# The first modulation rows as four 32-column tiles, with all tokens normed first

## The chip, the cores and the metric

The kernel runs on one core of one Trainium2 chip. The metric is the device time in microseconds (us) of one execution, the median of several runs. The core has five engines that run side by side and wait for one another through semaphores: PE (TensorE: matrix products and transposes), DVE (VectorE), ACT (ScalarE), POOL (GpSimd) and SP (SyncE). In this kernel SP issues nearly all transfers, one after the other in its queue, and ACT issues some small ones.

## The reference, cut to what matters

One inference step of a two-layer diffusion trunk: 512 latent tokens and 128 context tokens, width 1024, float32. Layer 0 is neighbourhood attention, layer 1 grouped-query attention; each is followed by a gated feed-forward part with a width-3 convolution. Everything that the change touches is the start of layer 0, up to its values:

```python
def adaln(cond, w, b):
    m = jax.nn.silu(cond) @ w + b
    return jnp.split(m[..., None, :], 6, axis=-1)
...
        sh_ap, sc_ap, g_ap, sh_fp, sc_fp, g_fp = adaln(c_ctx, ada_w[l], ada_b[l])
        sh_as, sc_as, g_as, sh_fs, sc_fs, g_fs = adaln(c, ada_w[l], ada_b[l])
        hp = rmsnorm(xp, norm_mix_pre[l]) * (1.0 + sc_ap) + sh_ap
        hs = rmsnorm(xs, norm_mix_pre[l]) * (1.0 + sc_as) + sh_as
        if l % N_MIXERS == 0:
            qp, kp, vp = na_qkv(hp, na_w_qkv[i])
...
            qs, ks_, vs = na_qkv(hs, na_w_qkv[i])
```

So two condition vectors (one for latents, one for context) are multiplied with a 1024 x 6144 matrix. The first 2048 columns of the result are the shift and the scale of the first norm. With them the normed tokens become the input of the query, key and value products.

## The kernel before

All names below are those of the code. Tokens are held as five tiles of 128 (`NT`), four latent and one context. The width of 1024 is eight blocks of 128 (`KC`).

**The first stage** does four things. It loads the five token tiles and norms them (`x_load`, `x_norm`: square on ACT, two small POOL operations, scaling on DVE). It transposes them on PE into `xT` (`x_turn`, eight transposes a tile). It forms the shift and scale (`mod_load`, `mod_rows`, `mod_cols`) and applies them to `xT`. The scaled result is held twice: `hT[0]` is rounded to the reduced type F32R, which PE multiplies in one pass, and `hT[1]` is the remainder. Last come the values of the first four heads (`v_part`), in three products for each block: high by high, high by low, low by high.

**The modulation goes in four groups** (`i` = 0 to 3). Group `i` holds 256 columns of the shift and 256 of the scale, which belong to two of the eight blocks of `xT`. Its weights are four tiles of 128 x 4 x 256 numbers, 512 KB each. A constant string says what becomes of each tile: `r` keeps it in float32 and multiplies it by `stf` (the conditions in float32, four stationary columns), `p` and `d` split it by `wsplit` into a rounded part (a cast on ACT) and a remainder (a subtraction, on POOL for `p`, on DVE for `d`), and multiply both parts by `st` and `st2`:

```python
ADA0 = "rrpdprdr" * 2
```

`mod_rows(i)` leaves four rows of 512 numbers in one PSUM bank; ACT copies them out as `rs`. `mod_cols(i)` multiplies pieces of `rs` by the small selector `sel`, which turns rows into columns and adds up the pieces, then forms `gcol` and `hcol` on DVE and scales: ACT writes `hT[0]`, DVE overwrites `xT` and subtracts to get `hT[1]`. `v_part(i, cs)` then uses the two blocks of group `i` for the token tiles in `cs`: six products for each of them.

**The order.** PE keeps the order in which the code issues its instructions (`mm`, `turn` and `pe` chain them). The other engines' order is made by a scheduler that follows the code's order as priority. Buffers carry a tag with a number of copies; a load into a tag waits until one of its buffers is given back, and all later loads in SP's queue wait behind it. Today the raw tiles have six buffers (`wf`), and the splits draw on four shared ones (`wr`, `wh`, `wl`), which the value and query-key weights of the next stage use too. The value weights are loaded by `wv_load` between the groups.

**What follows.** `crs` are convolution weights, loaded on ACT's queue and turned on PE just ahead of the last `v_part`. The next stage, neighbourhood attention, begins with query-key products (PE records named `qk`), builds bias tables for each head on POOL (`tb`, from transfers named `tr`), and fills PE's time with the later modulation rows (`ada_work`, records named `ada`), which already use four stationary tiles of 32 columns:

```python
for j in range(4):
    mm(ps[32 * j : 32 * j + 32, 0:256], scolp[:, 2 * kk : 2 * kk + 32], raw[:, 256 * j : 256 * j + 256],
       start=kk == 0, stop=kk == KC - 1)
```

`scolp` holds the conditions of block k in columns 2k and 2k + 1; of the 32 columns that a tile reads from there, only the first two are used.

Of the kernel before, what the change touches and what calls it, by code (L numbers as in the profile page):

```python
# [9 lines left out]
F32 = mybir.dt.float32  # L10
# [31 lines left out]
NC = 3  # L42
QKH = (slice(0, 256), slice(256, T))
CTX = 2
ADA0 = "rrpdprdr" * 2
ORDER = "a f a f p0 t0 a s0 f s1 t1 a f v0 t2 a a f a v1 f p1 f a a s2 a s3 v2 f f f a a p2 f f".split()
ORDER2 = "t0 p0 s0 s1 f a f a f f t1 v0 t2 a a f a f f a a p1 v1 s2 a f a s3 f v2 f p2 a f f".split()
PRO = 19
# [43 lines left out]
def hybrid_step(ctx: ExitStack, tc: tile.TileContext, A, O):  # L92
# [10 lines left out]
    def mm(*a, **k):  # L103
        pe(nc.tensor.matmul(*a, **k))  # L104
# [4 lines left out]
    def f32(t):  # L109
        return t.bitcast(F32)  # L110
# [39 lines left out]
    def wsplit(src, a, b, low=None, own=None, pin=False):  # L150
        q = own or wp
        raw = q.tile([P, a, b], F32, tag="wr", name="wr")
        nc.sync.dma_start(raw, src)
        hi = q.tile([P, a, b], F32R, tag="wh", name="wh")
        i = nc.scalar.copy(hi, raw)  # L155
        lo = q.tile([P, a, b], F32R, tag="wl", name="wl")
        j = (low or nc.vector).tensor_sub(lo, raw, f32(hi))  # L157
        if pin:
            tc.keep_in_program_order(i)
            tc.keep_in_program_order(j)  # L160
        return hi, lo

    def rows(w, r0, nr, c0, ncol):
        return w[r0 * P : (r0 + nr) * P, c0 : c0 + ncol].rearrange("(k p) n -> p k n", p=P)
# [282 lines left out]
    vts_of = {}  # L447
    with ExitStack() as s:
        sp = s.enter_context(pool("st"))
        sel = sp.tile([4, 2], F32, name="sel")  # L450
        nc.sync.dma_start(sel, A["k_sel"])
        xts = []

        def x_load(t):
# [11 lines left out]
        colb = sp.tile([P, 24], F32, name="colb")  # L466
        nc.vector.tensor_copy(colb, ct[:, 16:40])
        bk.put(ct)
        st = sp.tile([P, KC, 4], F32R, name="st1")
        st2 = sp.tile([P, KC, 4], F32R, name="st2")  # L470
        stf = sp.tile([P, KC, 4], F32, name="stf")
        nc.vector.tensor_copy(st2, zero_f.unsqueeze(2).broadcast_to([P, 8, 4]))
        nc.vector.tensor_copy(stf, zero_f.unsqueeze(2).broadcast_to([P, 8, 4]))
        for q in range(2):
            sc8 = scol[:, 8 * q : 8 * q + 8]
            nc.vector.tensor_copy(st[:, :, 2 * q], sc8)
            nc.vector.tensor_copy(st2[:, :, 2 * q], sc8)
            nc.vector.tensor_copy(stf[:, :, 2 * q], sc8)
            nc.vector.tensor_copy(scolp[:, q : 2 * KC : 2], sc8)
            nc.vector.tensor_sub(st[:, :, 2 * q + 1], sc8, f32(st[:, :, 2 * q]))  # L480
        xT = sp.tile([P, KC, T], F32, name="xT")
        gcol = sp.tile([P, KC, 2], F32, name="gcol")
        hcol = sp.tile([P, KC, 2], F32, name="hcol")
# [20 lines left out]
                bk.put(tr)  # L504

        def mod_load(i):
            out = []
            for j in range(4):
                src = rows(A["ada_w"][0], 4 * (j % 2), 4, D - D * (j // 2) + 256 * i, 256)
                how = ADA0[4 * i + j]  # L510
                if how == "r":
                    raw = sp.tile([P, 4, 256], F32, tag="wf", name="wf", bufs=6)
                    nc.sync.dma_start(raw, src)
                    out.append((raw,))
                else:
                    out.append(wsplit(src, 4, 256, nc.gpsimd if how == "p" else None))
            return out

        def mod_rows(i, ws):

            row = bk.get("row")
            for j, w in enumerate(ws):
                rv = row[0:4, 256 * (j // 2) : 256 * (j // 2) + 256]
                for k in range(4):
                    kk = 4 * (j % 2) + k
                    for x, y in zip((stf,) if len(w) == 1 else (st, st2), w):
                        mm(rv, x[:, kk, :], y[:, k, :], start=kk == 0 and y is w[0],
                           stop=kk == KC - 1 and y is w[-1])
            rs = sp.tile([4, 512], F32, tag="rs", name="rs")
            nc.scalar.copy(rs, row[0:4, :])  # L530
            bk.put(row)
            return rs

        def mod_cols(i, rs):

            col = bk.get("col")
            for n in range(4):
                mm(col[:, 2 * n : 2 * n + 2], rs[:, n * P : n * P + P], sel, start=True, stop=True)
            cv = col[:, 0:8].rearrange("p (a b) -> p a b", b=2)
            ks = slice(2 * i, 2 * i + 2)  # L540

            def bc(c0):
                return colb[:, c0 + 2 * i : c0 + 2 * i + 2].unsqueeze(2).broadcast_to([P, 2, 2])

            nc.vector.scalar_tensor_tensor(gcol[:, ks, :], cv[:, 0:2, :], 1.0, bc(8), op0=ALU.add, op1=ALU.add)
            nc.vector.tensor_mul(gcol[:, ks, :], gcol[:, ks, :], bc(16))
            nc.vector.tensor_add(hcol[:, ks, :], cv[:, 2:4, :], bc(0))
            bk.put(col)
            for k in (2 * i, 2 * i + 1):
                for q, cs in ((0, slice(0, NS)), (1, slice(NS, T))):  # L550
                    g1, h1 = gcol[:, k, q : q + 1], hcol[:, k, q : q + 1]
                    nc.scalar.activation(hT[0][:, k, cs], xT[:, k, cs], AF.Identity, bias=h1, scale=g1)
                    nc.vector.tensor_scalar(xT[:, k, cs], xT[:, k, cs], g1, h1, op0=ALU.mult, op1=ALU.add)
                nc.vector.tensor_sub(hT[1][:, k, 0:T], xT[:, k, :], f32(hT[0][:, k, 0:T]))
# [7 lines left out]
        def x_in_norm(ts):  # L562
            for t in ts:
                x_load(t)
                x_norm(t)

        x_in_norm((0, 1))
        loads[0] = mod_load(0)
        x_in_norm((2, 3, 4))
        for i in range(2):  # L570
            loads[i + 1] = mod_load(i + 1)
            wv_load(i)
# [16 lines left out]
        rs = mod_rows(0, loads[0])  # L589
        for t in range(NT):  # L590
            x_turn(t)
        mod_cols(0, rs)
        for i in range(1, 4):
            rs = mod_rows(i, loads[i])
            v_part(i - 1, (0, 1))
            mod_cols(i, rs)
            v_part(i - 1, (2, 3, 4))
        crs = []
        for l in range(2):
            cr = sp.tile([2 * FC, 4, P], F32, name=f"cr{l}")  # L600
            nc.scalar.dma_start(cr[:, 0:3, :], A["ffn_conv_w"][l].rearrange("j (n p) -> n j p", p=P))
            nc.scalar.dma_start(cr[:, 3, :], A["ffn_conv_b"][l].rearrange("(n p) -> n p", p=P))
            crs.append(cr)
# [1220 lines left out]
```

## Time and profile before

| what | value |
|---|---|
| median of 3 runs | 1701.52 us (1698.48 to 1703.72) |
| the profiled execution's own time | 1699.22 us |
| its span, first to last instruction | 1697.4 us |
| mean granted clock of PE | 0.974 |
| share of the span in which PE / DVE / ACT / POOL is busy | 94 / 61 / 53 / 44% |
| moved by DMA | 242.43 MB, 143 GB/s on average |
| the first stage, up to the first query-key product | 0 to 74.06 us |

The profiled execution is one of its own; its time is to be set beside the median before a sum made in it is turned into a forecast. In the views, L104 and L107 are helpers through which every matrix product and transpose goes, so there the tile's name (`row`, `col`, `vp`, `qk`, `tr`) tells the groups apart. L157 is the subtraction of a split and L155 its cast; L153 issues a split's load; L552 to L554 are the scaling. A float32 product shows as two records. Times stand in us, the mean of one instruction in ns.

### The profile page before, as it was taken

The page shows a single profiled execution, that of the slowest core. Times are in us where ns is not written, and L with a number is a line of the kernel's source. Part 1 is how long each engine was busy: PE and PEld are TensorE (multiplying, and loading weights), DVE is VectorE, ACT ScalarE, POOL GpSimd, SP SyncE. Part 2 cuts the span into 40 slices and gives each one's busy share as a digit, 9 for nine tenths or more (in the row PEclk, how much of TensorE's full clock was granted, in tenths as well). Part 3 has the DMA queues.
Part 4 walks back from the last instruction along what each step waited for, and adds up shares of the span by engine and source line. Part 5 has one row for each costly group of instructions (what it writes and reads, how often), then busy time and mean ns, then how long its engine had stood idle before and what let it go on. Part 6 is the DMA issues. An engine that isn't in the chain of part 4 may idle for free.

```text
span 1697.4 us, 26300 instructions
## 1 busy us (share of the span) xinstructions
PE 1589.7 (94%) x9709; PEld 1376.1 (81%) x9709; DVE 1039.7 (61%) x1725; ACT 903.6 (53%) x1721; POOL 751.7 (44%) x651
## 2 busy tenths in 40 slices
PE   6899998999999899989979888999998999998998
PEld 3788897977988788988868666777887999997876
DVE  4444454557875555672375776775696788784264
ACT  5466657655554444553355444664555665663353
POOL 3544545444245354442344345442424555652253
PEclk9999999989999999999989998999999999999999
DMA  9544544116376576347557410001636333336574
GB/s 269 150 112 121 141 127 118 32 63 224 113 235 203 189 218 185 121 153 236 161 187 232 133 38 13 2 1 63 211 112 188 115 120 98 117 117 212 174 238 170
DMA packets 193220, 242.43 MB, mean 143 GB/s; under 512 B 11108, under 2 KB 149572, under 8 KB 193092
## 3 DMA queue, kind: packets, MB, share of 16 engines
q1 hardware_dynamic: 182232, 233.13, 43.7%
q10 hardware_dynamic: 10860, 7.62, 2.3%
q8 instruction: 76, 1.25, 0.3%
q14 instruction: 52, 0.43, 0.1%
HBM read 214.38 MB, written 26.34 MB: 142 GB/s over the span
## 4 chain that ended last, share of the span: by engine, by line
PE 58%; DVE 13%; DMA 8%; POOL 7%; ACT 6%; issue 6%; ACTq 1%; SPq 0%; POOLq 0%; DVEq 0%
PE acc L104 17%; PE ux L104 10%; PE y L104 5%; PE uz L104 4%; PE po L104 3%; PE s L104 3%; DMA wr<-in_ada_w 3%; PE tp L107 3%; PE qk L104 3%; PE uy L104 3%; PE vp L104 3%; DMA wr<-in_na_w_qkv 2%; POOL wl L1117 2%; DVE t L1193 2%; PE ada L104 2%
## 5 line engine op out<-in xcount | busy, mean ns | idle before, releaser
L157 POOL TENSOR_TENSOR wl<-wr,wh 128x1024 fp32r<-128x1024 f32 x80 | 196.3, 2457 | 279.6 <-ACT wh L155 274.9
L1117 POOL TENSOR_TENSOR wl<-wr,wh 128x1024 fp32r<-128x1024 f32 x80 | 194.7, 2451 | 68.7 <-ACT wh L1116 59.3
L104 PE MATMUL ux<-B,wh 128*128 128x322 f32 x832 | 201.9, 313 | 1.9 <-DVE B L210 1.8
L1193 DVE SCALAR_TENSOR_TENSOR t<-C,cw,t 128x644 f32<-128x644 f32 x176 | 156.6, 890 | 55.8 <-ACT t L1191 54.9
L104 PE MATMUL acc<-wh,alo 128*128 128x512 f32 x440 | 175.5, 399 | 10.7 <-DVE alo L1086 10.7
L104 PE MATMUL acc<-wh,ahi 128*128 128x512 f32 x440 | 175.6, 399 | 9.5 <-DVE act L1204 9.5
L155 ACT CAST wh<-wr 128x1024 fp32r<-128x1024 f32 x148 | 153.5, 1047 | 45.0 <-DMA wr<-in_na_w_qkv 17.5
L104 PE MATMUL acc<-wl,ahi 128*128 128x512 f32 x440 | 174.7, 397 | 0.0
L104 PE MATMUL uz<-B,wh 128*128 128x322 f32 x640 | 158.4, 315 | 0.0
L104 PEld LDWEIGHTS ux<-B,wh 128*128 128x128 f32 x832 | 143.6, 189 | 9.6 <-issue 3.3
L1086 DVE TENSOR_TENSOR alo<-ain,ahi 128x384 fp32r<-128x384 f32 (+1 forms) x88 | 55.1, 631 | 141.8 <-ACT ahi L1084 141.8
L104 PE MATMUL ux<-B,wl 128*128 128x322 f32 x416 | 129.2, 311 | 0.0
L1084 ACT CAST ahi<-ain 128x384 fp32r<-128x384 f32 (+1 forms) x88 | 40.5, 462 | 166.3 <-PE acc L104 139.8
L104 PE MATMUL qk<-hT,wh 128*128 128x384 f32 (+1 forms) x512 | 126.6, 320 | 0.4 <-DVE qs L799 0.4
L104 PEld LDWEIGHTS uz<-B,wh 128*128 128x128 f32 x640 | 111.6, 190 | 6.6 <-issue 3.7
L1117 POOL TENSOR_TENSOR vl<-wr,vh 128x1024 fp32r<-128x1024 f32 x38 | 96.5, 2540 | 34.2 <-ACT vh L1116 34.2
L104 PEld LDWEIGHTS acc<-wh,alo 128*128 128x128 f32 x440 | 84.4, 192 | 30.4 <-DVE alo L1086 11.9
L1116 ACT CAST wh<-wr 128x1024 fp32r<-128x1024 f32 x88 | 89.5, 1049 | 35.0 <-DVE wr L1140 33.6
L104 PEld LDWEIGHTS acc<-wh,ahi 128*128 128x128 f32 x440 | 84.6, 192 | 28.4 <-issue 10.2
L1191 ACT ACTIVATE t<-C,cw 128x644 f32<-128x644 f32 x88 | 78.7, 894 | 50.7 <-DVE C L1221 47.4
L157 DVE TENSOR_TENSOR wl<-wr,wh 128x1024 fp32r<-128x1024 f32 x68 | 91.1, 1353 | 21.5 <-ACT wh L155 21.0
L104 PE MATMUL uz<-B,wl 128*128 128x322 f32 x320 | 100.0, 313 | 0.5 <-POOL wl L1117 0.4
(264 smaller groups left out, 4193.8 us busy)
## 6 DMA issues: line engine op xcount, KB each, us to landing
wr<-in_ada_w SPq DMA_DIRECT2D x88, 512.0 KB
wr<-in_ffn_w_up SPq DMA_DIRECT2D x88, 512.0 KB
wr<-in_ffn_w_down SPq DMA_DIRECT2D x88, 512.0 KB
act<-act SPq DMA_DIRECT2D x44, 321.0 KB
wr<-in_na_w_qkv SPq DMA_DIRECT2D x24, 512.0 KB
mod<-modrow SPq DMA_DIRECT2D x20, 512.0 KB
ain<-act SPq DMA_DIRECT2D x44, 192.0 KB
xres<-xo SPq DMA_DIRECT2D x15, 512.0 KB
```

The source lines that it names most:

```text
L104: pe(nc.tensor.matmul(*a, **k))
L107: pe(nc.tensor.transpose(*a, **k))
L155: i = nc.scalar.copy(hi, raw)
L157: j = (low or nc.vector).tensor_sub(lo, raw, f32(hi))
L1084: nc.scalar.copy(hi[:, 0 : c1 - c0], ain[:, 0 : c1 - c0])
L1086: nc.vector.tensor_sub(lo[:, 0 : c1 - c0], ain[:, 0 : c1 - c0], f32(hi[:, 0 : c1 - c0]))
L1116: nc.scalar.copy(hl[0], src)
L1117: low.tensor_sub(hl[1], src, f32(hl[0]))
L1191: nc.scalar.activation(t, taps(0), AF.Identity, bias=cw[:, 3, n : n + 1], scale=cw[:, 1, n : n + 1])
L1193: nc.vector.scalar_tensor_tensor(t, taps(d), cw[:, w, n : n + 1], t, op0=ALU.mult, op1=ALU.add)
```

## The change

All five token tiles are loaded and normed first, ahead of the first modulation weights. The sixteen weight tiles are no longer split: they are loaded as float32 into seven `wf` buffers and multiplied as they are. In a group, the four products of a tile go to four column tiles of 32 (partitions 32j to 32j + 31), so block k's part lands in rows 32j and 32j + 1 with j = k mod 4. The row bank is copied with all 128 partitions, and `sel` now has 128 rows and adds up the four tiles; it is made by a reduction of the identity instead of a load. The operands `st`, `st2` and `stf` go.

The order on PE becomes: all transposes, rows 0, rows 1, columns 0, rows 2, columns 1, values 0 (two token tiles), columns 2, values 0 (the other three), values 1, rows 3, values 2 (three tiles), columns 3, values 2 (two), values 3. Before, it was: rows 0, transposes, columns 0, and then for each further group its rows, two tiles of the values before, its columns, three tiles. The convolution loads move into `wf` buffers.

```diff
-ADA0 = "rrpdprdr" * 2
...
-        sel = sp.tile([4, 2], F32, name="sel")
-        nc.sync.dma_start(sel, A["k_sel"])
+        sel = sp.tile([P, 2], F32, name="sel")
+        nc.vector.tensor_reduce(sel, ident.rearrange("p (j q) -> p q j", q=32)[:, 0:2, :], axis=AX.X, op=ALU.add)
...
         def mod_load(i):
-            out = []
-            for j in range(4):
-                src = rows(A["ada_w"][0], 4 * (j % 2), 4, D - D * (j // 2) + 256 * i, 256)
-                how = ADA0[4 * i + j]
-                if how == "r":
-                    raw = sp.tile([P, 4, 256], F32, tag="wf", name="wf", bufs=6)
-                    nc.sync.dma_start(raw, src)
-                    out.append((raw,))
-                else:
-                    out.append(wsplit(src, 4, 256, nc.gpsimd if how == "p" else None))
+            out = {}
+            for n in range(2):
+                for h in range(2):
+                    out[n, h] = sp.tile([P, 4, 256], F32, tag="wf", name="wf", bufs=7)
+                    nc.sync.dma_start(out[n, h], rows(A["ada_w"][0], 4 * h, 4, D - D * n + 256 * i, 256))
             return out
...
             row = bk.get("row")
-            for j, w in enumerate(ws):
-                rv = row[0:4, 256 * (j // 2) : 256 * (j // 2) + 256]
-                for k in range(4):
-                    kk = 4 * (j % 2) + k
-                    for x, y in zip((stf,) if len(w) == 1 else (st, st2), w):
-                        mm(rv, x[:, kk, :], y[:, k, :], start=kk == 0 and y is w[0],
-                           stop=kk == KC - 1 and y is w[-1])
-            rs = sp.tile([4, 512], F32, tag="rs", name="rs")
-            nc.scalar.copy(rs, row[0:4, :])
+            for (n, h), w in ws.items():
+                for j in range(4):
+                    k = 4 * h + j
+                    mm(row[32 * j : 32 * j + 32, 256 * n : 256 * n + 256], scolp[:, 2 * k : 2 * k + 32],
+                       w[:, j, :], start=h == 0, stop=h == 1)
+            rs = sp.tile([P, 512], F32, tag="rs", name="rs")
+            nc.scalar.copy(rs, row)
...
-        x_in_norm((0, 1))
+        x_in_norm(range(NT))
         loads[0] = mod_load(0)
-        x_in_norm((2, 3, 4))
...
-        rs = mod_rows(0, loads[0])
         for t in range(NT):
             x_turn(t)
-        mod_cols(0, rs)
-        for i in range(1, 4):
-            rs = mod_rows(i, loads[i])
-            v_part(i - 1, (0, 1))
-            mod_cols(i, rs)
-            v_part(i - 1, (2, 3, 4))
+        rs = mod_rows(0, loads[0])
+        for i in range(1, 3):
+            nxt = mod_rows(i, loads[i])
+            mod_cols(i - 1, rs)
+            rs = nxt
+        v_part(0, (0, 1))
+        mod_cols(2, rs)
+        v_part(0, (2, 3, 4))
+        v_part(1, range(NT))
+        rs = mod_rows(3, loads[3])
+        v_part(2, (0, 1, 2))
+        mod_cols(3, rs)
+        v_part(2, (3, 4))
         crs = []
         for l in range(2):
-            cr = sp.tile([2 * FC, 4, P], F32, name=f"cr{l}")
+            cr = sp.tile([2 * FC, 4, P], F32, tag="wf", name="cr", bufs=7)
```

More of the change, by code (lines that the diff above doesn't have):

```diff
@@ L468, in hybrid_step @@
         bk.put(ct)
[L469 to L473, printed above, removed]
-        for q in range(2):
[L475 to L480, printed above, removed]
+        for q in range(2):
+            nc.vector.tensor_copy(scolp[:, q : 2 * KC : 2], scol[:, 8 * q : 8 * q + 8])
         xT = sp.tile([P, KC, T], F32, name="xT")
```

## The prediction

> **What bounds the kernel now.** The page comes first: where does the profiled execution spend its span, and on which engine?
>
> ```profile
> span 1697.4 us, 26300 instructions
> PE 1589.7 (94%) x9709; PEld 1376.1 (81%) x9709; DVE 1039.7 (61%) x1725; ACT 903.6 (53%) x1721; POOL 751.7 (44%) x651
> ```
>
> PE is busy for 94% of 1697.4 us, so over the whole span only PE work, or a stretch in which PE waits, can give time. The diff touches only the first stage, so the windows of that stage come next (columns: length, busy time of PE, weight loads, DVE, ACT, POOL, then granted clock, DMA share, GB/s).
>
> ```profile
> 0.00:20.00 20.00, 7.89 (x27) 2.84 (x28) 4.78 (x18) 7.09 (x12) 4.20 (x11) 1.00 0.88 228
> 20.00:40.00 20.00, 17.55 (x123) 12.64 (x123) 13.15 (x22) 12.91 (x22) 6.99 (x8) 1.00 1.08 341
> 40.00:45.00 5.00, 5.00 (x29) 2.24 (x28) 4.23 (x3) 3.70 (x7) 3.99 (x2) 1.00 0.22 60
> 55.00:60.00 5.00, 5.00 (x24) 3.27 (x24) 2.73 (x6) 2.92 (x4) 1.59 (x1) 0.59 0.36 105
> ```
>
> The memory moves 228 and then 341 GB/s for 40 us and collapses to 60 GB/s at 40 to 45 us, although modulation weights are still missing. The queue's own waits say why, and the chain of waits shows what the end of the stage then hangs on.
>
> ```profile
> SPq L153 <- POOL wl L157: 13.8, 5, 6.4
> SPq L153 <- DVE wl L157: 9.8, 3, 4.9
> 42.78 0.37 SPq L153 DMA_DIRECT2D wr<-in_ada_w  x1
> ```
>
> ```profile
> 3.00 5.31 DMA x<-in_x_sample
> 30.74 8.37 DMA wr<-in_na_w_qkv
> 43.61 3.40 DVE wl L157
> 57.25 6.47 PE row L104 x32
> 63.72 1.61 PE vp L104 x12
> ```
>
> The load queue waits 13.8 + 9.8 us for the subtractions of the split (L157) to give back a buffer, so the third load of the last weight group is only issued at 42.78. The chain runs through that split (3.40 us) and through the row products (6.47 us), which PE also executes at a granted clock of 0.59. The stage is thus bound by split, buffers and row products, not by the memory. That is what the change removes.
>
> **The change part by part.** I read four durations from the timeline (start, length) and the groups by shape.
>
> ```profile
> 61.83 1.89 PE L104 MATMUL row<-wf,stf 128*4 128x256 f32 x8
> L104 PE MATMUL ada<-wr,scolp x640: 376/403/637, 100.5 to 1309.0; 128*32 128x256 f32 x160
> 100.54 0.57 PE ada L104 x8
> L157 DVE TENSOR_TENSOR wl<-wr,wh 128x1024 fp32r<-128x1024 f32 x4 | 7.4, 1858 | 4.4 <-ACT wh L155 4.4
> L155 ACT CAST wh<-wr 128x1024 fp32r<-128x1024 f32 x14 | 14.6, 1042 | 9.2 <-DMA wr<-in_ada_w 4.0 <-PE row L104 2.4 <-PE vp L104 1.5
> ```
>
> *Row products.* One raw weight tile (four products, 8 records) costs 1.89 us with four stationary columns. The later modulation rows (`ada`) already use four 32-column tiles on the same 128x256 shape, and there 8 records take 0.57 us, with other work directly before and behind. The change gives all 16 tiles this form: 16 x 0.57 = 9.1 us, against 8 x 1.89 = 15.1 us for today's raw half alone. One stage of rows becomes 4 x 0.57 = 2.3 us.
>
> *Splits.* Half of the 16 tiles are split today: 8 casts of 1.04 us on ACT go, four subtractions of 1.86 us on DVE go, and four on POOL. The 16 tiles then take seven raw buffers, each given back by PE as soon as its four products have run.
>
> *Landing times.* Every large load is 512 KB, 0.524 MB. By 40 us the two windows moved 0.228 x 20 + 0.341 x 20 = 11.4 MB: 21 loads (five x, fourteen modulation, two value weights; 11.0 MB) and 0.4 MB of small ones. In the new order the fifth x is load 5, groups 0 to 3 end with loads 9, 13, 18 and 23. By the same rates: load 5 (3.0 MB) at 13.1, load 9 (5.1 MB) at 21.6, load 12 (6.7 MB) at 26.2, load 18 (9.8 MB) at 35.4, load 23 (12.4 MB) at 43.1 us. This needs a queue that never runs dry. With seven buffers, the eighth modulation load waits until PE has eaten the first tile, and PE reaches that only behind all transposes.
>
> ```profile
> 19.46 1.06 ACT L489 ACTIVATE junk<-x 128x1024 bf16<-128x1024 f32 x1 [1.22 <-DMA x<-in_x_sample]
> 21.56 0.75 DVE L491 TENSOR_SCALAR x<-x,rstd 128x1024 f32<-128x1024 f32 x1 [1.70 <-POOL rstd L178]
> 20.73 1.04 PE L107 MATMUL tr<-ident,x 128*128 128x128 f32 x8
> ```
>
> A landed token tile is normed 2.9 us later (19.46 to 22.31) and turned in 1.04 us: 13.1 + 2.9 + 1.0 = 17.0, first tile eaten at 17.6. Seven tiles are queued until 26.2, so the wait hides with 8 us to spare. Behind this load on the in-order queue stand all later weights; if the cover went, each would slip by the overrun.
>
> *The path.* Now the order on PE: rows 1, columns 0, rows 2, columns 1, values 0 in two pieces around columns 2, values 1, rows 3, and so on. What a stage of columns and of scaling costs, I take from the last stage of today, which runs undisturbed:
>
> ```profile
> 65.26 1.05 PE L104 MATMUL col<-sel,rs 4*128 4x2 f32 x8
> 70.14 0.82 DVE L554 TENSOR_TENSOR hT<-xT,hT 128x640 fp32r<-128x640 f32 x1
> 73.94 0.28 PE L104 MATMUL vp<-wh,hT 128*128 128x256 f32 x1
> 74.06 0.28 PE L104 MATMUL qk<-hT,wh 128*128 128x256 f32 x1
> ```
>
> Columns take 1.05 us; 4.65 us after them the low half is ready (66.31 to 70.96); columns to the first query-key product is 65.26 to 74.06, 8.80 us. A value product costs 1.61 / 12 = 0.134 us, so 18 are 2.4 and 30 are 4.0 us.
> Rows 2 end at 35.4 + 0.6 = 36.0. Columns 1 end at 37.0. Values 0 with columns 2 between end at 37.0 + 1.6 + 1.05 + 2.4 = 42.1. Values 1 also need the scaling of columns 1, at 37.0 + 4.65 = 41.7. There a collision has to be priced:
>
> ```profile
> 32.97 2.35 POOL L157 TENSOR_TENSOR wl<-wr,wh 128x1024 fp32r<-128x1024 f32 x1 [4.33 <-ACT wh L155]
> 33.04 2.96 DVE L554 TENSOR_TENSOR hT<-xT,hT 128x640 fp32r<-128x640 f32 x1
> ```
>
> The same DVE subtraction takes 2.96 us when a POOL subtraction starts beside it, against 0.82 us alone: 2.1 us more. The second value weight lands as load 19 at 36.9; its POOL subtraction then runs at about 38 to 40.5, on top of this scaling. I count one collision: 43.8 us.
> The Trainium skill, "SBUF — State Buffer" (its lines on the shared port pair), says why: the pair is an exclusive lock, held for a whole instruction, so a two-input DVE operation fully blocks beside GpSimd. The trace agrees (2.96 against 0.82 us); by that rule every such pairing costs up to a POOL instruction, and two more could meet the query and key weights, 4 us in all.
> Then values 1 to 47.8 (46.1 without the collision), rows 3 (landed at 43.1) to 50.1, the scaling of columns 2 is ready by about 48.5 to 50.6, values 2 for three tiles to 52.5, and 8.80 us more: **61.3 us instead of 74.06, a gain of 12.8 us**; 59.6 us and 14.5 without the collision. The best end is the memory: load 23 at 43.1 + 0.6 + 2.4 + 8.8 = 54.9, a gain of 19.2. I take 13, since the collision falls in the middle of the scaling.
>
> *Small parts.*
>
> ```profile
> L530 ACT COPY rs<-row 4x512 f32<-4x512 f32 x4 | 2.3, 572 | 4.9 <-PE row L104 4.9
> L503 ACT COPY xT<-tr 128x512 f32<-128x512 f32 x5 | 2.8, 571 | 0.7 <-PE tr L107 0.7
> 10.44 0.75 DVE L491 TENSOR_SCALAR x<-x,rstd 128x1024 f32<-128x1024 f32 x1 [4.69 <-POOL rstd L178]
> 1.22 0.58 ACTq L601 DMA_DIRECT2D cr<-in_ffn_conv_w  x1
> L104 PEld LDWEIGHTS vp<-wh,hT 128*128 128x128 f32 x80 | 14.1, 209 | 4.6 <-DVE hT L554 3.5 <-issue 0.9
> L104 PEld LDWEIGHTS col<-sel,rs 4*128 4x128 f32 x32 | 4.2, 199 | 0.6 <-DVE xT L501 0.2
> ```
>
> The row copy now has 128 partitions: 0.571 against 0.572 us, nothing. The added reduction of `ident` and the dropped casts and selector load lie in front of DVE's 4.69 us of idleness: nothing, and at most 0.75 us without that cover. The column products now load 128 rows instead of 4: a load of 4*128 took 0.199 us, the nearest of 128*128 took 0.209, so nothing; at most their own 1.05 us again in each of the two stages on the path. There is one buffer for the copied rows, so the copy of rows 1 waits on ACT until columns 0 have read the last one, with casts and scaling behind it: PE runs these columns next, so 1.05 us at a time when the path waits for memory anyway. The convolution loads move from 1.22 us to behind a freed raw buffer. On ACT's queue the scaling and casts stand behind that issue; rows 2 free it at 36, so I take nothing, and up to 2.3 us if rows 3 must.
>
> *Does it carry?* Query and key weights are loads 24 to 26, 44.6 to 47.7 us, and split by about 53, ahead of 61. From the last value product on, code and buffers are as before, and the next stage waits on itself only. So I carry the gain in full: 1699.2 (profiled time, 1.8 above its span) - 13 = 1686.2. The median of the runs, 1701.5, lies 2.3 above the profiled one: 1688.5.
>
> **Rivals.** *A slower clock on the path.* The first rows show it:
>
> ```profile
> 12.40 6.44 PE L104 MATMUL row<-wf,stf 128*4 128x256 f32 x16 [7.83 <-DMA wf<-in_ada_w]
> 47.06 0.28 PE L104 MATMUL row<-wl,st 128*4 128x256 f32 x1 [1.92 <-DVE wl L157]
> ```
>
> 16 records in 6.44 us are 0.40 each, against 1.89 / 8 = 0.24 later: 1.7 times as long, though the granted clock of that window reads 1.00. In the new order PE works in short bursts until 36 us, one tile per load. If it then stays slow, the path's PE share (1.05 + 4.0 + 2.3 + 2.4 + 1.05 + 3.1 = 13.9 us) grows by 70%, 9.7 us; half of that is 4.9. The 0.59 window could come back as well. Time: 1693 to 1698. Against it: once fast, PE stayed so through a gap of 1.92 us (the record behind it takes 0.28, as those before).
> The Trainium skill, "TensorE: Matmul & The Clock Gate", Part 1, gives this as a rule: half clock by default, full after about 3.4 us of sustained work, half again after an idle window of that length. The trace agrees with slow rows first and fast ones later, its ratio is 1.7.
> *The gain is swallowed.* The next stage's first scores wait on tables:
>
> ```profile
> 80.82 3.45 DMA tr<-in_k_rpb
> 93.11 0.59 PE s L104
> ```
>
> If these held their place, the scores would stay at 93.11 and nearly all would be lost: 1700 to 1702. Against it: the tables' memory is this stage's own, and comes free with the last scaling.
> *Slower: loads in lockstep.* If buffers come back late, each of the nine loads beyond seven buffers and the two value loads lands only after the one before is eaten, 5.31 us apiece as for the first x: 22 + 11 x 5.3 = 80, + 0.6 + 2.4 + 8.8 = 92, 18 us late: 1719. For it: the queue waits above. It decides once rows 0 start after 26.2 us; I have 17.0.
>
> **How the numbers follow.** Forecast 0.72, slow clock 0.13, swallowed 0.08, lockstep 0.07. 0.3% is 5.1 us, about what a measurement of this kernel can tell from none: 1696.4. Faster: the forecast and 0.10 of the clock, 0.82. Same: 0.03 and 0.08, 0.11. Slower 0.07. The range runs from the memory's end (1682.3, and 1 us of spread) to the slow clock's end, 1698; left out are swallowed and lockstep, 0.15.
>
> **What would show it.** Right: DMA above 300 GB/s without a gap from 10 to 43 us; no L157 on DVE; 8 row records in about 0.6 us; first query-key product at 59 to 62 us instead of 74.06; the later stages the same distance from it. Wrong: the load queue waiting for PE's rows before 26 us with a DMA hole behind it, value products over 0.2 us, DVE's scaling still over 6 us a stage, or first scores near 93 us despite early values.

## The result, and the profile after

The changed kernel takes 1688.64 us (median of 19 runs, 1681.61 to 1697.53), beside 1701.11 us (19 runs, 1694.41 to 1705.66) for the kernel before on the same chip: a ratio of 0.9933 [0.9916, 0.995], 12.5 us less. The forecast was 1688.5, faster. The number was hit; the way to it was not quite the one foreseen: the first stage gave about 3 us less than forecast, and the median fell by about 3 us more than the stage.

The profiled execution after took 1692.79 us, 1.8 above its span. Its head and the windows of the first stage (columns as before: length, PE, weight loads, DVE, ACT, POOL, granted clock, DMA share, GB/s):

```profile
span 1691.0 us, 26261 instructions
PE 1582.7 (94%) x9709; PEld 1376.5 (81%) x9709; DVE 1032.1 (61%) x1712; ACT 895.3 (53%) x1713; POOL 740.2 (44%) x647
```

```profile
20.00:25.00 5.00, 3.42 (x53) 1.72 (x51) 1.07 (x2) 1.17 (x2) 0.00 (x0) 1.00 1.10 349
25.00:30.00 5.00, 3.71 (x31) 1.75 (x23) 0.00 (x0) 0.00 (x0) 0.00 (x0) 0.61 1.09 347
30.00:35.00 5.00, 2.69 (x19) 0.87 (x19) 2.63 (x5) 3.72 (x6) 2.08 (x1) 0.50 1.09 348
40.00:45.00 5.00, 5.00 (x25) 5.00 (x25) 1.71 (x6) 3.99 (x7) 2.36 (x1) 0.50 1.16 315
55.00:60.00 5.00, 4.45 (x39) 4.06 (x38) 2.40 (x8) 2.30 (x4) 1.80 (x1) 1.00 0.65 206
```

The hole in the transfers is gone: 315 GB/s at 40 to 45 us, where the kernel before moved 60. A slow clock now stands in the middle of the stage: the granted clock of PE is 0.50 to 0.61 from 25 to 45 us, where the kernel before had 1.00. The load queue's own waits on the row products:

```profile
SPq L500 <- PE row L103: 5.5, 6, 2.4
```

These 5.5 us in six waits leave no gap in the transfers, since the other loads were queued in time. The 23.6 us in which the modulation loads waited for subtractions of the split are gone with the split. The chain that ended last, in order of time (start, length):

```profile
26.41 10.16 DMA wf<-in_ada_w
36.62 1.08 PE row L103 x8
37.70 1.80 PE col L103 x8
39.50 2.77 PE vp L103 x12
42.27 1.51 PE col L103 x8
43.80 0.16 DVE gcol L528
...
48.76 2.35 DVE xT L536
51.13 2.91 DVE hT L537
54.09 1.81 PE vp L103 x13
55.89 0.80 PE col L103 x8
```

Until 36.62 us the path is a landing, then PE's products, and from 43.80 to 54.09 VectorE's scaling, in which two operations take 2.43 and 2.90 us where their like take 0.34 and 0.82 (shown below; the chain counts the part of each that lies on it). The stage ends here (start of the first of 512 products):

```profile
L103 PE MATMUL qk<-hT,wh x512: 276/334/689, 64.5 to 325.6; 128*128 128x256 f32 x86, 128*128 128x384 f32 x85
```

64.5 us instead of 74.06: the stage gives 9.6 us, of 12.8 forecast.

### The profile page after: what moved, and what is told of

It is laid out like the page before. It is cut to its first block, busy times and chain, and to the rows that moved or that the text cites. A ratio compares the mean times of both kernels' runs of the same rounds, so it can differ in the third digit from the quotient of the medians.

```text
span 1691.0 us, 26261 instructions
## 1 busy us (share of the span) xinstructions
PE 1582.7 (94%) x9709; PEld 1376.5 (81%) x9709; DVE 1032.1 (61%) x1712; ACT 895.3 (53%) x1713; POOL 740.2 (44%) x647
## 4 chain that ended last, share of the span: by engine, by line
PE 57%; DVE 15%; POOL 7%; DMA 7%; issue 7%; ACT 6%; SPq 1%; ACTq 1%; POOLq 0%; DVEq 0%
PE acc L103 17%; PE ux L103 9%; PE y L103 5%; PE uz L103 4%; PE po L103 4%; PE qk L103 4%; PE s L103 4%; PE tp L106 3%; DMA wr<-in_ada_w 3%; PE vp L103 3%; PE uy L103 2%; DVE t L1181 2%; POOL wl L1105 2%; PE ada L103 2%; DVE al L1105 2%
## 5 line engine op out<-in xcount | busy, mean ns | idle before, releaser
L156 POOL TENSOR_TENSOR wl<-wr,wh 128x1024 fp32r<-128x1024 f32 x76 | 185.7, 2446 | 282.3 <-ACT wh L154 276.8
L1105 POOL TENSOR_TENSOR wl<-wr,wh 128x1024 fp32r<-128x1024 f32 x80 | 194.7, 2451 | 69.7 <-ACT wh L1104 66.4
L154 ACT CAST wh<-wr 128x1024 fp32r<-128x1024 f32 x140 | 145.1, 1048 | 33.8 <-DMA wr<-in_na_w_qkv 17.4
L1104 ACT CAST wh<-wr 128x1024 fp32r<-128x1024 f32 x88 | 89.5, 1049 | 34.1 <-DVE wr L1128 32.7
L103 PEld LDWEIGHTS acc<-wl,ahi 128*128 128x128 f32 x440 | 84.5, 192 | 18.5
```

What stands on the lines that cost most here:

```text
L1104: nc.scalar.copy(hl[0], src)
L1105: low.tensor_sub(hl[1], src, f32(hl[0]))
```

## The experiments

"Stage end" is always the start of the first query-key product; "scaling 3" is the end of the last subtraction of the scaled tokens, which the last value products wait for. Each kernel was timed against the kernel before on its chip, 1698.01 us for the first group (again, old_order, split_new, narrow), 1698.18 for the second (two_bufs, warm, cols_two, and the single run before_two), 1698.84 for the last (free, free_warm, vector_low, rows_first).

**The changed kernel once more (again), and the kernel before once more (before_two).** No edit; they tell what of the two traces is chance.

> The changed kernel as it is, for a second trace. In the first one PE's granted clock fell to 0.5 between 27 and 46 us, the value products of the first pieces took 0.21 us each instead of 0.12, and the stage ended at 64.5 us where 61.3 were forecast. If the slow stretch belongs to the new order (short bursts of rows, one tile per load), it comes back at the same place and the stage ends within 1 us of 64.5. If it is chance of one execution, the rows of groups 1 and 2 take about 0.6 us a tile here and the stage ends at 61 to 62. The time is 12 to 13 us below the kernel before either way; the 3 us lost between the stage's end (9.6 us early) and the end of the span (6.4 early) should not come back if they are the clock's chance dips in the first feed-forward part.

> The kernel before once more, for a second trace. In the first the stage ended at 74.06 us, with a granted clock of 0.73 and 0.59 between 50 and 60 us. The changed kernel's median is 12.5 to 13.2 us lower, but its stage ends only 9.6 us earlier than in that trace. If the first trace of before is typical, the stage ends at 73 to 75 us again and the other 3 us must lie in later stages; if the slow window is sometimes longer, it ends at 76 us or later and explains them.

Again: 1684.83 us, 0.9926 [0.9901, 0.995], stage end 64.6. The slow clock recurs (0.90 at 25 to 30 us, 0.50 from 30 to 40, 0.73 to 45), so in both executions it belongs to this order of work. Before_two: one run, 1704.29, stage end 74.3. The stage's gain is thus 9.6 us in one pair of traces and 9.7 in the other.

**Part one alone: the new weights in the old order (old_order).**

```diff
 (from the changed kernel)
-        x_in_norm(range(NT))
+        x_in_norm((0, 1))
         loads[0] = mod_load(0)
+        x_in_norm((2, 3, 4))
...          PE: rows 0 ahead of the transposes, then per stage
+            rs = mod_rows(i, loads[i])
+            v_part(i - 1, (0, 1))
+            mod_cols(i, rs)
+            v_part(i - 1, (2, 3, 4))
```

> Float32 weights, seven buffers and four column tiles as in the change, but the order of the kernel before: two token tiles loaded ahead of the first weights, rows 0 ahead of the transposes, and each group's rows just ahead of two tiles of the values before. Theory (the gain comes from weights that no longer wait for a split, and from short rows; the order is worth little): loads stay above 300 GB/s until about 43 us, the stage ends at 57 to 62 us, and the time is within 4 us of the changed kernel's, 1685 to 1691. Rival (the gain comes from having three quarters of the rows ahead of the values): the stage ends at 69 us or later and the time is 1695 or more.

Measured: 1693.06 us, 0.9964 [0.9944, 0.9984]; stage end 69.3. Of the stage's 9.6 us this leaves 4.8, of the ratio's gain about half. The theory that the order is worth little fell; the stage ended where the rival had it (69 us or later). The queue's waits, the last loads of the rows, and one window:

```profile
SPq L500 <- PE row L103: 13.8, 3, 10.1
```

```profile
30.43 15.18 SPq L500 DMA_DIRECT2D wf<-in_ada_w  x4
```

```profile
40.00:45.00 5.00, 5.00 (x31) 4.32 (x35) 3.53 (x9) 2.29 (x4) 0.00 (x0) 0.50 0.14 45
```

The code keeps PE's order, and there the rows of group 2 stand behind values 0, which wait for the scaling. So raw buffers are held, the last group's four loads are issued over 15.18 us, and the transfers fall to 45 GB/s. Seven buffers did not suffice with values ahead of rows.

**Part two alone: the old split weights in the new order (split_new).**

```diff
 (from the kernel before: the changed kernel's two lists of order)
+        x_in_norm(range(NT))
...
+        for i in range(1, 3):
+            nxt = mod_rows(i, loads[i])
+            mod_cols(i - 1, rs)
+            rs = nxt
...
```

> The kernel before with its splits and four stationary columns, but with the new order of loads and products. Theory (unsplit weights carry the gain): the load queue still waits for subtractions, the memory falls under 200 GB/s somewhere before 45 us, the stage ends at 72 to 80 us, and the time is 1699 to 1707, no gain. Rival (the order carries it): the stage ends at 66 us or earlier and the time is 1688 to 1693.

Measured: 1702.59 us, 1.002 [1.0003, 1.0038]; stage end 76.9. As the theory had it: the order alone gives nothing, and loses a little.

```profile
SPq L153 <- POOL wl L157: 18.2, 6, 6.3
```

```profile
40.00:45.00 5.00, 3.10 (x15) 1.74 (x15) 2.93 (x1) 1.72 (x2) 5.00 (x2) 0.66 0.41 121
```

The queue still waits 18.2 us for GpSimd's subtractions, and the hole (121 GB/s) stays.

**Unsplit weights, new order, but one column tile (narrow).**

```diff
-                    mm(row[32 * j : 32 * j + 32, 256 * n : 256 * n + 256], scolp[:, 2 * k : 2 * k + 32],
-                       w[:, j, :], start=h == 0, stop=h == 1)
+                    mm(row[0:32, 256 * n : 256 * n + 256], scolp[:, 2 * k : 2 * k + 32],
+                       w[:, j, :], start=k == 0, stop=k == 7)
```

The copy of the row bank and `sel` go down to 32 rows with it.

> The changed kernel with one column tile instead of four: all eight blocks of a group go to the first 32 columns, one after the other. Everything else stays, float32 loads and order too. The theory that the column tiles matter only because rows stand in front of everything: a tile costs 1.89 us (3.2 us while PE is slow) instead of 0.57, more than the 1.54 us in which a tile lands, so PE and no longer the memory sets the pace of rows 0 to 2: they end 8 us later, rows 3 add 5.3 us on the path, the stage ends at 74 to 80 us and all of the gain is gone, 1699 to 1706. Rival (loads alone carry the gain, PE has slack): rows 3 alone are late, the stage ends near 70 us and the time is 1692 to 1695.

Measured: 1692.88 us, 0.9963 [0.9945, 0.998]; stage end 73.0. Beside again in the same group the stage loses 8.4 us and the time 8.0. The stage went the theory's way, though its end lies 1 us under the 74 to 80 expected: it keeps 1.1 us of the 9.6. The time lies in the rival's range, 5.1 us below the kernel before, more than the stage alone gives; what lies behind the stage is taken up at the end of the next section.

```profile
21.79 14.00 PE L103 MATMUL row<-wf,scolp 128*32 128x256 f32 x64
```

64 records, 8 raw tiles, take 14.00 us, 1.75 a tile. Loads land every 1.5 us (below), so the rows are now slower than the memory; the queue waits 14.7 us for them. PE was busy for all of 20 to 65 us, and its granted clock reads 1.00 there. With four tiles PE is faster than the memory and waits for it, and in both traces of that kernel its clock falls.

**Two raw buffers instead of seven (two_bufs).** The edit is `bufs=7` to `bufs=2` in both places (weights and convolution loads); it brings the prediction's lockstep rival about.

> The changed kernel with two raw buffers instead of seven, to put a price on the load queue standing still (the lockstep case, which was priced at 5.3 us a load and 18 us in all for one load in flight). The third weight load now waits for the first tile of rows, at about 20.5 us, so the memory stands still from about 16 to 20 us, and then two loads are in flight. If a load's way from issue to landing is 4 to 5 us, two in flight give 210 to 270 GB/s, the twelve tiles up to group 2 end at about 45 us instead of 36.6, and the stage ends at 72 to 76 us: time 1696 to 1702. If the queue was not what held the kernel before and other work hides such a wait, the stage ends below 68 us and the time stays under 1692.

Measured: 1711.04 us, 1.0069 [1.0044, 1.0095]; stage end 88.6. Slower than the kernel before, and far worse than the 72 to 76 us I had expected for the stage.

```profile
SPq L500 <- PE row L103: 28.5, 12, 11.4
```

```profile
68.80 0.94 SPq L500 DMA_DIRECT2D wf<-in_ada_w  x2
```

The loads go out in pairs about 6 us apart (from 28.24 to 52.98), so rows 2 end at 54.8 us, not at 45 as expected. The last pair is issued only at 68.80: it needs buffers that the first tiles of rows 3 give back, and these stand behind values 1 in PE's order, which the expectation forgot. The rival's mechanism exists, then; with seven buffers it does not occur.

**PE kept busy between the rows (warm).** Products of `ident` into a bank that is overwritten later, three after a tile of groups 1 and 2, six at the start of rows 2.

```diff
+        def keep_warm(n):
+            for _ in range(n):
+                mm(vb[0][:, 256 : 256 + P], ident, ident, start=True, stop=True)
...
+            keep_warm(6 if i == 2 else 0)
...
+                keep_warm(3 if i in (1, 2) and (i, n, h) != (2, 1, 1) else 0)
```

> The changed kernel with added products that nobody reads, to keep PE from slowing down while it waits for loads: three 128x128 products of the identity behind each weight tile of groups 1 and 2 (not behind the last), and six between columns 0 and rows 2. In both traces of the changed kernel PE's granted clock is 0.5 from about 27 to 43 us; columns 1 and 2 take 1.87 us instead of 1.05, the first value products 0.21 instead of 0.12, and VectorE, which keeps its order, sits for 2.3 us on the columns of group 2 with the scaling of group 1 queued behind them. If the slow clock costs time on the path, the rows of group 2 end 0.5 us earlier, columns 1 another 0.8, columns 2 start 2 to 3 us earlier, and the stage ends at 60 to 62 us instead of 64.5, the time at 1682 to 1686 beside 1685 to 1689. If the path is memory and VectorE alone, it ends within 1 us of 64.5; if the added products are in the way, later.

Measured: 1686.02 us, 0.9933 [0.9912, 0.9954]; stage end 65.0. The clock is 1.00 until 60 us, and yet nothing is won. VectorE's rows and one window:

```profile
40.89 2.28 DVE L535 TENSOR_TENSOR gcol<-gcol,colb 128x4 f32<-128x4 f32 x1
47.56 2.45 DVE L542 TENSOR_SCALAR xT<-xT,gcol,hcol 128x128 f32<-128x128 f32 x1
50.04 2.90 DVE L543 TENSOR_TENSOR hT<-xT,hT 128x640 fp32r<-128x640 f32 x1
```

```profile
60.00:65.00 5.00, 4.59 (x26) 4.60 (x27) 2.02 (x7) 1.74 (x8) 3.28 (x6) 0.66 0.25 80
```

A new collision of 2.28 us (a 4-column operation that takes 0.16 alone, beside a subtraction on GpSimd from 40.74 to 43.15) eats most of the lead. Scaling 3 ends 1.1 us earlier (60.35 instead of 61.45). Then PE's clock falls after all, to 0.66 for the last products. Of the two outcomes expected the second came: the slow clock alone is not the path.

**Columns 2 ahead of all of values 0 (cols_two).** This takes away VectorE's wait for columns 2.

```diff
-        v_part(0, (0, 1))
         mod_cols(2, rs)
-        v_part(0, (2, 3, 4))
+        v_part(0, range(NT))
```

> The changed kernel with columns 2 directly behind columns 1, ahead of all values 0 instead of behind two tiles of them. VectorE works in order and has the small operations of columns 2 in front of most of the scaling of group 1, and waited 1.9 to 2.3 us for PE there. If this wait is on the path, columns 2 come 2 us earlier, the scaling of group 1 ends at 46 to 47 us instead of 48.8, and the stage ends at 62 to 63 us, the time 1.5 to 2.5 us below the changed kernel's. If the scaling's length alone decides, or PE's slow clock moves the loss elsewhere (values 0 then start 2 us later), the stage ends within 0.7 us of 64.5.

Measured: 1685.61 us, 0.9929 [0.9906, 0.9952]; stage end 68.2, scaling 3 at 62.6. A miss: columns 2 do come earlier (VectorE has them at 42.39 instead of 43.80), but the scaling then meets GpSimd worse, and the granted clock falls to 0.69 and 0.63 in the two windows from 60 to 70 us.

```profile
47.94 4.99 DVE L536 TENSOR_SCALAR xT<-xT,gcol,hcol 128x128 f32<-128x128 f32 x2
```

**The collisions taken away (free), and with PE busy as well (free_warm).**

```diff
+        if low == "none":
+            return hi, hi
...   for the second value weight and the first query and key weights
-            wv[i] = wsplit(rows(wqkv, 4 * i, 4, 2048, 256), 4, 256, nc.gpsimd)
+            wv[i] = wsplit(rows(wqkv, 4 * i, 4, 2048, 256), 4, 256, "none" if i else nc.gpsimd)
```

> The changed kernel with three remainders left out (second value weight of the first stage, first query and first key weight): the rounded part stands in for them, so neither POOL nor VectorE subtracts there and the products with the low half use the wrong operand, at the same cost. In the trace of the changed kernel the scaling of groups 1 and 2 on VectorE ran beside these POOL subtractions, and single operations took 2.43 and 2.90 us instead of 0.34 and 0.82. Theory (two limits side by side: PE's slow clock and these collisions): without collisions alone the scaling of group 2 ends at 50 us instead of 54.0, but PE, still slow, reaches values 2 only at 52.6, so the stage ends at 63 to 64.5 us. Rival (collisions alone are the path): it ends at 60 to 61.

> The three remainders left out as in the run beside it, and PE kept busy by the added products on the identity as in the earlier run. Each alone moves the stage's end by less than 1 us (the added products alone: 65.0 us). Theory (two limits side by side): together the scaling of group 2 ends at 47 to 49 us, values 1 end at about 47.5, rows 3 at 50, and the stage ends at 60 to 62 us, 3 us or more below the changed kernel. If something third holds the path, a load or the order on ACT, the stage stays at 63.5 us or later.

Both kernels leave out those three subtractions, so their results lack the low halves; they serve to time the rest. Free: 1684.07 us, 0.9922 [0.9902, 0.9942]; scaling 2 ends at 50.2 instead of 54.0, as expected, but scaling 3 at 61.94 and the stage at 67.5, later than in the changed kernel and than either outcome expected: PE's granted clock falls to 0.63 and 0.68 in the two windows from 60 to 70 us. Free_warm: 1684.32 us, 0.9923 [0.9902, 0.9944]; scaling 2 ends at 46.7, scaling 3 at 58.30, stage end 63.9.

```profile
45.89 0.83 DVE L545 TENSOR_TENSOR hT<-xT,hT 128x640 fp32r<-128x640 f32 x1
52.43 0.16 DVE L536 SCALAR_TENSOR_TENSOR gcol<-col,colb 128x4 f32<-128x4 f32 x1 [5.71 <-PE col L103]
57.49 0.81 DVE L545 TENSOR_TENSOR hT<-xT,hT 128x640 fp32r<-128x640 f32 x1
```

```profile
60.00:65.00 5.00, 5.00 (x27) 5.00 (x27) 2.16 (x8) 2.62 (x9) 1.75 (x3) 0.56 0.28 67
```

For scaling 3, the busy PE alone gives 1.1 us, the missing collisions alone -0.5, both together 3.1: the two limits lie side by side. With both gone VectorE waits 5.71 us for columns 3, which stand behind values 1 and rows 3 on PE; then PE waits for scaling 3 and its clock drops to 0.56 for the last products. So the stage's end misses the 60 to 62 us expected and moves by 0.6 us only: by the expectation's own words a third thing holds the path, here the order on PE. (A fourth subtraction on GpSimd, from 51.54, is still there, and beside it a 4-column operation takes 1.31 us instead of 0.16.)

**Nothing left out: VectorE subtracts those three remainders (vector_low), and rows 3 moved up (rows_first).** Both with the busy PE.

```diff
 (vector_low: the low halves of the second value weight and the first query and key weights)
-            wv[i] = wsplit(rows(wqkv, 4 * i, 4, 2048, 256), 4, 256, nc.gpsimd)
+            wv[i] = wsplit(rows(wqkv, 4 * i, 4, 2048, 256), 4, 256, None if i else nc.gpsimd)
 (rows_first: that, and after values 0)
-        v_part(1, range(NT))
         rs = mod_rows(3, loads[3])
-        v_part(2, (0, 1, 2))
+        v_part(1, (0, 1))
         mod_cols(3, rs)
-        v_part(2, (3, 4))
+        v_part(1, (2, 3, 4))
+        v_part(2, range(NT))
```

> A complete version: PE kept busy by the added products, and the same three subtractions on VectorE instead of POOL. VectorE then does 3 x 1.35 us more itself, against 2.1 to 2.4 us of waiting for each POOL subtraction. By the theory of the two limits the scaling of group 2 ends at about 51 us instead of 53 to 54, and the stage ends at 61.5 to 63.5 us, the time 1 to 3 us below the changed kernel's. If VectorE's own work is as bad as the waiting, it stays at 64 to 65.

> The same version with the last quarter of the rows ahead of values 1 too: rows 3 directly behind values 0, columns 3 after two tiles of values 1. The scaling of group 3 can then follow that of group 2 without waiting for PE. If VectorE's chain is the limit, it ends one scaling (4.4 us, and one subtraction of 1.35) after group 2, at about 57 us, values 3 end at about 60, and the stage ends 2 us or more ahead of the run beside it, the time at 1680 to 1684. If waiting for the last weights (landed at about 44 us) blocks PE at the head of its queue instead, the stage ends later than there.

Vector_low: 1685.28 us, 0.9929 [0.991, 0.9949]; stage end 64.3, in the worse of the two ranges expected (64 to 65); its clock is 0.73 and 0.58 in the two windows from 55 to 65 us, much as in free_warm. Rows_first: 1679.94 us (1674.32 to 1681.68), 0.9895 [0.9877, 0.9912]; scaling 3 ends at 53.38, stage end 57.4.

```profile
52.56 0.82 DVE L543 TENSOR_TENSOR hT<-xT,hT 128x640 fp32r<-128x640 f32 x1
```

```profile
60.00:65.00 5.00, 5.00 (x33) 5.00 (x32) 0.84 (x2) 0.76 (x2) 4.53 (x4) 1.00 0.13 40
```

Only here does the upstream gain arrive: columns 3 are ready as VectorE comes free, PE never waits from 40 to 70 us, and the clock stays at 1.00 to 75. It is 18.9 us below the kernel before. The order alone divides it from vector_low, in the same group: 5.3 us, with each of its six runs below each of the six there. Its interval lies wholly below that of the changed kernel, but overlaps the wider one of again (0.9901 to 0.995). Whether the new order would win as much without the busy PE and the moved subtractions was not run.

## Why the prediction was right, point by point

**The cause was right.** The splits held the load queue, and both halves of the diff are needed to free it: without unsplit weights all is lost (split_new, 1.002), without the four tiles or without the order about half (narrow 0.9963, old_order 0.9964). The prediction did not price the halves apart. It did name the order on PE, as the sequence to add up and as what gives back the first raw buffer; that values ahead of rows would hold the later ones, as in old_order, it did not see. In the stage alone the tiles count for more than half: narrow keeps 1.1 us of 9.6.

**The landings** fell nearly as forecast: 347 to 350 GB/s from 15 to 40 us without a gap, and the last tile of group 2, forecast at 35.4, is taken at 36.62, 1.2 us later. Between 10 and 15 us the memory moved 258 GB/s, less than the 300 named as a sign of being right. The transposes took longer than thought (the first eight 1.97 us instead of 1.04, next view), so rows 0 began at 20.48 and not at 17.0; the cover until 26.2 was wide enough for that.

**The clock was the mis-sized term.** The prediction had rows at 0.57 us a tile, columns at 1.05 and value products at 0.134, and gave a slow clock on the path 0.13.

```profile
10.60 1.97 PE L106 MATMUL tr<-ident,x 128*128 128x128 f32 x8 [6.24 <-DVE x L480]
20.48 1.93 PE L103 MATMUL row<-wf,scolp 128*32 128x256 f32 x32
24.63 0.64 PE L103 MATMUL row<-wf,scolp 128*32 128x256 f32 x8 [0.78 <-DMA wf<-in_ada_w]
26.14 1.08 PE L103 MATMUL row<-wf,scolp 128*32 128x256 f32 x8 [0.87 <-DMA wf<-in_ada_w]
35.11 1.08 PE L103 MATMUL row<-wf,scolp 128*32 128x256 f32 x8 [0.42 <-DMA wf<-in_ada_w]
37.63 1.87 PE L103 MATMUL col<-sel,rs 128*128 128x2 f32 x8
```

Tiles land 1.5 us apart (24.63 to 26.14), PE is busy for 0.64 of each 1.5 us, and from 26.14 the same 8 records take 1.08. Columns then take 1.87, a value product 0.23 (2.77 us for 12 in the chain above). Columns 1 end at 39.5 instead of 37.0, values 0 with columns 2 at 46.6 instead of 42.1. Of these 4.5 us 1.2 are the later landing, and some 3.3 the clock; the rival had set 4.9 for the whole path. In warm, with the clock at 1.00, columns 2 end at 40.66 us instead of 43.76. My argument against it, a gap of 1.92 us in the kernel before that left PE fast, did not carry: one gap after dense work says nothing of a long run of short bursts. The table in the Trainium skill, "TensorE: Matmul & The Clock Gate", Part 1, lets the clock fall after an idle window of some 3.4 us. From the first token transposes at 10.60 to the slow row at 26.14 no gap was longer than 0.9 us, so this trace does not agree with that: short bursts with short gaps were enough. That the gaps are what did it is shown by warm, where filling them kept the clock at 1.00; how small the busy share has to be, no run here shows.

**The scaling was sized right and placed wrong.** I had one collision on the path, of 2.1 us, on the scaling of columns 1. It did not occur: the second value weight's subtraction ran from 41.90 to 44.26, while VectorE stood waiting for columns 2, and cost it 0.13 us. Two others did, both on the scaling of columns 2 (a third, 2.08 instead of 0.34 us at 33.28, fell on that of columns 0, off the path):

```profile
33.28 2.08 DVE L536 TENSOR_SCALAR xT<-xT,gcol,hcol 128x128 f32<-128x128 f32 x1 [0.79 <-ACT hT L535]
41.90 2.36 POOL L156 TENSOR_TENSOR wl<-wr,wh 128x1024 fp32r<-128x1024 f32 x1 [6.63 <-ACT wh L154]
43.80 0.16 DVE L528 SCALAR_TENSOR_TENSOR gcol<-col,colb 128x4 f32<-128x4 f32 x1 [2.33 <-PE col L103]
47.63 5.71 POOL L156 TENSOR_TENSOR wl<-wr,wh 128x1024 fp32r<-128x1024 f32 x2 [3.37 <-ACT wh L154]
48.67 2.43 DVE L536 TENSOR_SCALAR xT<-xT,gcol,hcol 128x128 f32<-128x128 f32 x1
51.13 2.90 DVE L537 TENSOR_TENSOR hT<-xT,hT 128x640 fp32r<-128x640 f32 x1
```

GpSimd's two subtractions for the first query and key weights run from 47.63 to 53.34; beside them VectorE takes 2.43 instead of 0.34 and 2.90 instead of 0.82, 4.2 us. This is the "two more could meet the query and key weights, 4 us in all" of the prediction, which I had named with the port lock of the Trainium skill's "SBUF — State Buffer" (shared port pair) and left out of the sum. The trace agrees with that rule for the two-input subtraction (2.90 us); the other held operation, 2.43 us, takes one tensor, which my sentence on the rule did not cover. The scaling of columns 1 was late too (47.3, forecast 41.7 to 43.8), for a reason I had not seen: VectorE's order puts the conversion of columns 2 ahead of most of it, so it waited 2.33 us for columns 2. Scaling 2 ended at 54.0 instead of 48.5 to 50.6.

**The stage's end**, 64.5, lies 3.2 us behind the forecast 61.3. Rows 3 end at 52.7 instead of 50.1: the 4.5 us of landing and clock, less the 1.7 us on the path of the collision that did not occur, less 0.2 by which values 1 and rows 3 are shorter. Scaling 2 ends another 1.3 us later (the collisions), PE waits 0.6 us for it, and columns 3 start at 55.73 instead of 52.5. From there to the end it is 8.8 us, as forecast (8.80). In free_warm, with both causes gone, scaling 3 ends at 58.30, close to the forecast's own 52.5 + 1.05 + 4.65 = 58.2 (columns 3 start 1.1 us ahead of it, as the priced collision is gone too, and the fourth subtraction takes 1.15 back). Of the prediction's signs of being wrong, two showed: value products over 0.2 us (0.23), and a scaling over 6 us long (columns 2, from 43.80 to 54.0); the first query-key product also missed its 59 to 62 us. So the mechanism was right, and the size of the stage's gain was not.

**The gain is carried:** the first scores start at 83.6 us instead of 93.1 and later work moves with them; swallowed and lockstep did not occur. But the stage's 9.6 us are 3 short of the measured 12.5, so that the forecast hit to 0.1 us is luck in part: a stage forecast 3 us too good met a median that fell 3 us more than the stage. One trace cannot show where those lie, because the same program varies by more:

```profile
412.00:752.00 340.00, 324.45 (x2278) 293.13 (x2277) 227.12 (x317) 176.25 (x261) 151.08 (x92) 0.98 0.56 174
```

```profile
412.00:752.00 340.00, 322.69 (x2291) 290.67 (x2290) 233.31 (x322) 179.45 (x265) 152.98 (x92) 1.00 0.58 180
```

The first is the changed kernel's profile, the second that of again: one program, at a granted clock of 0.98 and 1.00. From the first feed-forward projection to the first down product it takes 339.0 us in the one and 330.3 in the other (334.0 and 333.4 in the two traces of before). Such dips are why the one trace after has gained only 6.4 us of span. Taken over all profiles, the stretch from the stage's end to the start of the last down product is 1615.7 to 1620.9 us in the three with split weights (before, before_two, split_new) and 1606.6 to 1619.3, mean 1611.2, in the eleven with unsplit ones. In all eleven, too, the median gained more (or lost less) than the stage of the one trace, by 0.2 to 8.2 us. So some us seem to be won behind the stage, in code that the diff does not touch. Among these traces the two longest stretches (1619.3 in after, 1620.9 in before_two) have a granted clock of 0.97 and all others 0.98, but a better clock of the changed kernel is not shown: over whole runs on one chip it averages 0.971 in the six of again, against 0.975 in 28 of the kernel before. What wins them stays open; 9.6 us alone lie inside both intervals of the ratio (8.5 to 14.3 us for the changed kernel, 8.5 to 16.8 for again).

## What to carry to other kernels

When a transfer hole is traced to buffers held by a slow consumer, look at two things at once: what is done to the data before the buffer is free, and what stands ahead of that work on its engine. Here the new order without unsplit weights gave nothing, and unsplit weights without the new order gave half. A stage freed from its memory is then bound by whatever waits in order next (here VectorE's scaling, beside GpSimd, and PE's columns), and taking away one of two limits side by side shows next to nothing: undo them together before calling one harmless, and expect a third behind them, as here the order of rows 3. And when PE is to work in short bursts in a new schedule, do not price its products at the rate of the old one.

## What the runs showed of the hardware

- The granted clock of PE fell to 0.50 although no gap since the first token tile's transposes was longer than 0.9 us, with 0.64 us of work in each 1.5 us; with dummy products between the tiles (warm) it stayed at 1.00 to 60 us.
- In warm, cols_two, free, free_warm, vector_low and old_order PE waits for the last scaling late in the stage, its clock falls to 0.56 to 0.73 in the window behind, and the products that were waited for run slow: there a wait costs more than its length. In the changed kernel itself, with waits of 0.55 and 1.08 us there, it stayed at 1.00.
- The 8 row records of a raw tile take 0.48 us on four column tiles when four such tiles follow one another (1.93 us for 32 records), and 1.75 on one 32-column tile, 3.6 times as long. One tile by itself takes 0.64 us on four column tiles and 1.89 with four columns.
- Beside GpSimd's subtraction, VectorE's operations with one tensor are held as well as those with two: 0.34 us became 2.43, a pair of them 4.99, and a 4-column operation of 0.16 us took 2.28.
